# Inverse roots with fewer VectorE steps, row norms by halves on two engines, and two weight units of the odd layer split early into kept buffers

## The chip, the cores and the metric

The kernel runs on one core of one Trainium2 chip. The metric is the device time of an execution in microseconds (us), the median of three runs. The profile is of one further execution of the same kernel.

## The reference

The program is one inference step of a two-layer trunk, all in float32. It works on 128 context tokens (`x_prompt`) and 512 latent tokens (`x_sample`), each a row of 1024 values.

```
for l in 0, 1:
    six shift/scale/gate vectors from silu(c) for the latent rows, silu(c_ctx) for the context rows
    h = rms_norm(x, norm_mix_pre) * (1 + scale1) + shift1
    l = 0:  y = even_mixer(h)      # gated linear attention beside retention, one output projection
    l = 1:  y = mla_mixer(h)       # latent attention, 8 heads
    x = x + gate1 * rms_norm(y, norm_mix_post)
    h = rms_norm(x, norm_mlp_pre) * (1 + scale2) + shift2
    y = square(relu(h @ w_mlp1)) @ w_mlp2        # 1024 -> 4096 -> 1024
    x = x + gate2 * rms_norm(y, norm_mlp_post)

def rms_norm(x, g):
    return x * rsqrt(mean(x ** 2) + 1e-6) * g

def mla_mixer(h, ...):
    q_lat, ckv, kpe = split(h @ w_in_odd, (256, 256, 64))
    q   = rms_norm(q_lat, q_a_norm) @ w_q_b      # 8 heads of 128 + 64 (64 turned by position)
    ckv = rms_norm(ckv, kv_a_norm)               # keys and values: ckv @ w_kv_b, kpe
    ...                                          # cached keys joined, softmax, @ w_out_odd
```

It returns both sets of rows, the context's `ckv` and `kpe`, and the scan states.

## The kernel before

**Tiles.** The 640 token rows are five row tiles of 128; tile 0 is the context, tiles 1 to 4 are the latent rows. Activations `x`, `y` are 128x1024. The normed and modulated rows are turned on TensorE (`ps<-ident,y` in the trace) and kept as `hT`, 128 columns of tokens by eight blocks of 128 features (k-blocks).

**Products.** A float32 product is made of three: each operand is split into a high part (rounded to the type fp32r) and a low part (the rest), and `mm3` issues high by high, high by low, low by high. In the trace `hT_91` and `hT_92` are the two parts of the turned rows.

**Weights.** `plan` writes one list of all weight units, `wlist`, in the order in which they are wanted. `weights` walks it: for each unit it takes one of three load buffers (pool `raw`) and issues the load on SP's DMA queue. `weight_rooms` walks it behind, and takes a destination (usually from the pool `w` of ten buffers, otherwise what a `room` of the unit returns). `weight_split` then casts on ScalarE (high part), subtracts on VectorE (low part), and gives the load buffer back. A unit's `prio` goes to the thread that splits it.

**Order.** The `Weave` planner keeps many threads (Python generators), each recording operations through `Engine` at line 269, which is why every instruction of the trace has the line L269. While the program is written, the planner simulates the engines with its own costs per operation and picks for each engine the ready operation of the lowest `prio`; on VectorE the older thread goes first among equals, on the other engines the one that was ready first. The result is a fixed order per engine. A thread waits for an `Event`, or for a buffer of a `Slots` pool.

**PSUM.** Eight banks are lent between the slots `psg` (products) and `psum` (transposes) with `w.give`.

**Roots.** An inverse root is made of a logarithm and an exponential on ScalarE, and one Newton step of three VectorE operations (`rsqrt`). Ahead of it one VectorE operation adds the epsilon to the sum of squares.

**Norms.** `pre_norm` takes the squares of a tile (ScalarE), the root, writes the normed rows `xn` (VectorE; in the MLP's tail `xn` is the finished tile's `y` buffer), and starts two halves that each turn four blocks, modulate them into `h` (VectorE for half 0, ScalarE for half 1) and split `h` into `hT`. `residual` takes the root of the output's norm and adds into `x`. `out_proj` ends the mixer with the residual and the norm of each tile, and `mlp` ends with a `tail` per tile: two halves of the output added to `y`, squared, gated, then `residual`; after the first MLP `pre_norm` follows for the odd layer, after the second the result is stored.

**Odd layer.** `odd` has two groups of products with `w_in_odd`: 256 columns (query latents, `q_tile`) and 320 columns (keys, values and rotary key, `kv_tile`). Each group has four weight units of two k-blocks, `u_in_odd`, so that a tile takes 24 products per group. The second group's units go to buffers that `odd` opens (`room1`, `room2`); the first group's go to `w`. `norm256` norms a 256-column row of either group, and its result is turned. `park_x` stores each `x` tile when its `hT` is ready, and `cache` loads and turns the cached keys. Then `w_q_b`'s rotary part follows (`pqp` in the trace, `qpe_tile`), three banks go from `psg` to `psum`, and the heads begin: `projections` runs `proj(h)` for eight heads beside `all_values`, `scores`, `turns`, `outputs` and `finish`.

Of the kernel before, what the change touches and what calls it, by code (L numbers as in the profile page):

```python
# [19 lines left out]
P = 128  # L20
# [311 lines left out]
class Trunk:  # L332
# [68 lines left out]


# [75 lines left out]
    def weights(self):  # L478

        loads = [Event() for _ in self.wlist]  # L480
        self.w.spawn(self.weight_rooms(loads))
        for item, load in zip(self.wlist, loads):
            if isinstance(item, Event):
                continue
            if len(item) == 3:
                yield from self.pair_load(item[0], item[1], load)
                continue
            src, shape = item[:2]
            raw, hr = yield from self.take(self.raw, [P] + shape, F32, "raw")
            parts = list(src(raw) if callable(src) else [(raw, src)])  # L490
            self.w.aside(lambda: [self.nc.sync.dma_start(a, b) for a, b in parts],
                         then=lambda at: self.w.set(load, (raw, hr, at)))
            yield

    def weight_rooms(self, loads):
        for item, load in zip(self.wlist, loads):
            if isinstance(item, Event):
                yield item
                continue
# [21 lines left out]
    def wp_room(self):  # L521
        h = yield from self.take2(self.wp, [P, 2, 512], F32R, "wh")
        return h[0][0], h[1][0], [x[1] for x in h]

# [281 lines left out]
    def pre_norm(self, t, x, xn, sm, mods, ready, halves=None):  # L806
# [4 lines left out]
        nc.scalar.activation(self.junk, x, AF.Square, accum_out=sm[:, 0:1])  # L811
        yield
        nc.vector.tensor_scalar(sm[:, 1:2], sm[:, 0:1], D * EPS, None, op0=ALU.add)
        yield
        yield from self.rsqrt(sm[:, 1:2], sm[:, 2:3], sm[:, 3:4], 1.0 / D)
        nc.vector.tensor_scalar(xn, x, sm[:, 2:3], None, op0=ALU.mult)
# [40 lines left out]
    def residual(self, x, yg, sm, dst=None):  # L857

        nc = self.nc
        nc.vector.tensor_scalar(sm[:, 6:7], sm[:, 4:5], sm[:, 5:6], D * EPS, op0=ALU.add, op1=ALU.add)  # L860
        yield
        yield from self.rsqrt(sm[:, 6:7], sm[:, 7:8], sm[:, 3:4], 1.0 / D)
# [19 lines left out]
    def run(self):  # L882
# [17 lines left out]
        self.ident = const("ident", [P, P])  # L900
        self.fold, self.wide = const("fold", [P, P]), const("wide", [P, KC, 34])
# [8 lines left out]
    def plan(self):  # L910
# [11 lines left out]
        self.u_in_odd = (self.nat_units(io["w_in_odd"][0], ODD_GROUPS[:1], pair=True)  # L922
                         + self.nat_units(io["w_in_odd"][0], ODD_GROUPS[1:], rooms=self.odd_rooms))
# [36 lines left out]
    def main(self):  # L960
# [9 lines left out]
        halves = [[Event(), Event()] for _ in range(2)]  # L970

# [72 lines left out]
    def out_proj(self, units, oready, gate, mods, parked, gfree):  # L1044
# [6 lines left out]
        def tail(t):  # L1051
# [4 lines left out]
            for half in range(2):  # L1056
                ps, hp = yield out[half][t]
                s = slice(half * 512, half * 512 + 512)
                nc.scalar.activation(self.junk[:, 0:512], ps, AF.Square, accum_out=sm[:, 4 + half:5 + half])
                nc.vector.tensor_mul(y[:, s], ps, gr[c][:, s])  # L1060
                self.drop(hp)
# [32 lines left out]
    def mlp(self, ph, l, ready, xs, gate, mods, gfree):  # L1094
# [36 lines left out]
        def tail(t, ev):  # L1131
# [4 lines left out]
            for half in range(2):  # L1136
# [5 lines left out]
                nc.scalar.activation(self.junk[:, 0:512], y[:, s], AF.Square, accum_out=sm[:, 4 + half:5 + half])  # L1142
                yield
                nc.vector.tensor_mul(y[:, s], y[:, s], gr[c][:, s])
# [9 lines left out]
            else:  # L1154
                yield from self.residual(x, y, sm)
                yield from self.pre_norm(t, x, y, sm, mods, out_ready)
# [728 lines left out]
    def odd(self, ph, ready, xs):  # L1885
# [68 lines left out]
        def norm256(v, sm, gain, y):  # L1954
            nc.scalar.activation(self.junk[:, 0:256], v, AF.Square, accum_out=sm[:, 0:1])
            yield
            nc.vector.tensor_scalar(sm[:, 1:2], sm[:, 0:1], 256 * EPS, None, op0=ALU.add)
            yield
            yield from self.rsqrt(sm[:, 1:2], sm[:, 2:3], sm[:, 3:4], 1.0 / 256)
# [82 lines left out]
        for _ in range(3):  # L2042
            w.give(self.psum, (yield self.psg))
# [108 lines left out]
        def projections():  # L2152
            for h in range(HC):
                yield from proj(h)

# [150 lines left out]
        for g in (projections, all_values, scores, turns, outputs, finish, out_rooms):  # L2306
# [56 lines left out]
```

## Time and profile before

| what | value |
|---|---|
| median of three runs | 1523.9 us (1523.51 to 1525.08) |
| profiled execution, its own time | 1522.98 us |
| its span, first to last instruction | 1521.2 us |
| TensorE matmuls (PE) busy | 1473.8 us, 97% of the span, 8587 instructions |
| TensorE weight loads (PEld) busy | 1308.4 us, beside PE |
| VectorE (DVE) busy | 1092.6 us, 72% |
| ScalarE (ACT) busy | 651.7 us, 43% |
| GpSimd (POOL) busy | 113.0 us, 7% |
| mean granted TensorE clock | 0.987 |
| HBM traffic over the span | 112 GB/s |

Busy time counts instructions that run, not those that wait. In a row of the trace the first number is the start in us from the span's start, the second the time that the row's instructions took or covered; then come engine, line, operation, output and inputs with their shapes, and how often. A bracket at the end gives the idle time of that engine just before, and the operation whose end released it. SPq is the DMA queue of SyncE. "Granted clock" is the share of full clock that TensorE got.

### The profile page before, as it was taken

What the parts mean: (1) busy time and instruction counts of PE and PEld (TensorE: products, weight loads), DVE (VectorE), ACT (ScalarE), POOL (GpSimd) and SP (SyncE); (2) the same over time, 40 slices, a digit from 0 to 9 for tenths busy, and PEclk for the clock granted to TensorE, in tenths of its full rate; (3) what the DMA queues carried; (4) which work ended last, traced back from release to release, by engine and by line L of the source; (5) the groups of instructions that cost most, each with busy time, mean ns of one, the idle gap of its engine ahead of it and who ended that gap; (6) DMA issues with size and microseconds to landing.
All of it is one profiled execution on the core that took longest, in us unless ns stands there. A gap on an engine that the chain in (4) does not pass through costs nothing.

```text
span 1521.2 us, 22996 instructions
## 1 busy us (share of the span) xinstructions
PE 1473.8 (97%) x8587; PEld 1308.4 (86%) x8587; DVE 1092.6 (72%) x2247; ACT 651.7 (43%) x1526; POOL 113.0 (7%) x133
## 2 busy tenths in 40 slices
PE   5999999999999999999997999999999999999997
PEld 2688888889899899899896989997889989988996
DVE  4464674757767877777868788885765869996776
ACT  3583533646433232233246366673654323332332
POOL 0000200101021021021010100000002000000000
PEclk8999999999999999999998999999999999999999
DMA  9546222133555444445414110104422223432332
GB/s 331 166 156 209 87 69 80 44 110 112 163 163 152 143 128 146 144 129 152 123 42 140 48 29 22 43 29 139 167 83 70 63 77 112 130 120 84 98 103 105
DMA packets 148176, 171.44 MB, mean 113 GB/s; under 512 B 12144, under 2 KB 92640, under 8 KB 148064
## 3 DMA queue, kind: packets, MB, share of 16 engines
q1 hardware_dynamic: 148064, 169.97, 36.4%
q8 instruction: 67, 1.10, 0.3%
q14 instruction: 45, 0.37, 0.1%
HBM read 161.36 MB, written 8.59 MB: 112 GB/s over the span
## 4 chain that ended last, share of the span: by engine, by line
PE 89%; DVE 4%; ACT 3%; DMA 2%; issue 1%; SPq 0%; DVEq 0%; ACTq 0%
PE p L269 55%; PE pg L269 19%; PE ps L269 13%; PE pqk L269 2%; DVE y L269 1%; PE pv L269 1%; ACT junk L269 1%; DVE sm L269 1%; DMA raw<-in_w_in_even 1%; DVE x L269 1%; DMA x<-in_x_sample 1%; DMA raw<-in_w_out_odd 1%; ACT h L269 0%; SPq L269 0%; DVE rope L269 0%
## 5 line engine op out<-in xcount | busy, mean ns | idle before, releaser
L269 PE MATMUL p<-wh,hid 128*128 128x512 f32 x1280 | 399.6, 391 | 0.0
L269 PEld LDWEIGHTS p<-wh,hid 128*128 128x128 f32 x1280 | 240.3, 188 | 49.3
L269 PE MATMUL p<-hT,wh 128*128 128x256 f32 (+1 forms) x1280 | 280.1, 310 | 0.0
L269 PE MATMUL pg<-wh,hT 128*128 128x512 f32 (+3 forms) x840 | 264.8, 389 | 0.0
L269 PE MATMUL p<-wl,hid 128*128 128x512 f32 x640 | 249.7, 390 | 0.0
L269 DVE TENSOR_TENSOR wl<-raw,wh 128x1024 fp32r<-128x1024 f32 (+3 forms) x141 | 167.9, 1195 | 73.8 <-ACT wh L269 73.4
L269 PEld LDWEIGHTS p<-hT,wh 128*128 128x128 f32 x1280 | 216.1, 190 | 0.8
L269 ACT CAST wh<-raw 128x1024 fp32r<-128x1024 f32 (+3 forms) x145 | 147.6, 1022 | 137.9 <-PE p L269 98.6
L269 PE MATMUL p<-hT,wl 128*128 128x256 f32 (+1 forms) x640 | 198.7, 310 | 0.0
L269 PEld LDWEIGHTS pg<-wh,hT 128*128 128x128 f32 x840 | 155.2, 190 | 32.3 <-issue 9.2
L269 DVE SCALAR_TENSOR_TENSOR ada<-rada,cT,ada 128x512 f32<-128x512 f32 x196 | 146.7, 778 | 0.0
L269 PE MATMUL pg<-wl,hT 128*128 128x512 f32 (+3 forms) x360 | 141.9, 394 | 0.0
L269 PEld LDWEIGHTS p<-wl,hid 128*128 128x128 f32 x640 | 120.3, 188 | 24.1
L269 DVE TENSOR_TENSOR y<-y,p 128x512 f32<-128x512 f32 x140 | 96.0, 686 | 58.1 <-PE p L269 57.3
L269 POOL TENSOR_TENSOR r<-r 128x384 f32<-128x384 f32 (+1 forms) x80 | 80.6, 1007 | 729.1 <-ACT hid L269 392.8
L269 PEld LDWEIGHTS p<-hT,wl 128*128 128x128 f32 x640 | 121.3, 190 | 0.0
L269 ACT ACTIVATE r<-p 128x384 f32<-128x384 f32 (+1 forms) x80 | 35.0, 438 | 157.1 <-PE p L269 157.1
L269 PE MATMUL p<-hT,wq 128*128 128x320 f32 x576 | 88.1, 310 | 0.0
L269 PEld LDWEIGHTS p<-hT,wq 128*128 128x128 f32 x576 | 85.5, 188 | 0.5
L269 PEld LDWEIGHTS pg<-wl,hT 128*128 128x128 f32 x360 | 68.7, 191 | 11.9 <-issue 2.5
L269 DVE TENSOR_TENSOR hid<-r,hid 128x384 fp32r<-128x384 f32 (+1 forms) x80 | 38.9, 487 | 46.4 <-POOL r L269 46.3
L269 ACT CAST wq<-tw 128x512 fp32r<-128x512 f32 x48 | 27.6, 618 | 71.0 <-DVE tw L269 61.7
(282 smaller groups left out, 2325.0 us busy)
## 6 DMA issues: line engine op xcount, KB each, us to landing
raw<-in_w_mlp SPq DMA_DIRECT2D x128, 512.0 KB, 4.1
rada<-in_w_ada SPq DMA_DIRECT2D x160, 256.0 KB, 3.2
rada<-in_w_ada SPq DMA_DIRECT2D x16, 512.0 KB, 8.7
raw<-in_w_in_even SPq DMA_DIRECT2D x16, 512.0 KB, 4.9
x<-in_x_sample SPq DMA_DIRECT2D x8, 512.0 KB, 7.0
gate<-gate SPq DMA_DIRECT2D x8, 512.0 KB, 4.5
raw<-in_w_out_even SPq DMA_DIRECT2D x8, 512.0 KB, 5.2
raw<-in_w_out_odd SPq DMA_DIRECT2D x8, 512.0 KB, 3.7
```

Source lines behind the costliest of these rows:

```text
L269: emit = lambda: real(*a, **k)
```

## The change

**Roots.** A new `root(v, add, r, t)` takes the mean of squares and adds the epsilon as the bias of the logarithm. The two ScalarE operations follow the squares without a VectorE operation between them. The Newton step is three VectorE operations as before, each with two operators, and reads mean plus epsilon in its first one. `squares` scales the squares so that their sum is the mean. `pre_norm`, `residual` and `norm256` use it; other users of `rsqrt` stay. Where a row's squares come in two halves, the epsilon is added to the first half's sum as soon as that is there, and the sum serves as the second half's `add`.

**Halves.** In the first MLP's tail `pre_norm` runs with `shared=True`: VectorE writes columns 0 to 511 of the normed rows, ScalarE columns 512 to 1023.

**Kept buffers.** A new item `(2, kept)` of `wlist` stands ahead of unit 2 of the first odd group: `weights` takes two of the three load buffers there as destinations (named `wr`) and hands them to units 2 and 3 of that group, which pass through the third. They are given back when their group's last tile has used them. All eight units of the odd input projection have `prio=-1`.

**Banks.** The three banks that go from `psg` to `psum` ahead of the heads are now given by a thread of its own, once head 0's projections are done.

```diff
+    def root(self, v, add, r, t):
+        nc = self.nc
+        nc.scalar.activation(t, v, AF.Ln, bias=add)
+        nc.scalar.activation(r, t, AF.Exp, scale=-0.5)
+        yield
+        nc.vector.scalar_tensor_tensor(t, v, add, r, op0=ALU.add, op1=ALU.mult)
+        nc.vector.scalar_tensor_tensor(t, t, -0.5, r, op0=ALU.mult, op1=ALU.mult)
+        nc.vector.scalar_tensor_tensor(r, t, 1.5, r, op0=ALU.add, op1=ALU.mult)
+
+    def squares(self, x, sm, n):
+        self.nc.scalar.activation(self.junk[:, 0:x.shape[-1]], x, AF.Square, scale=n ** -0.5, accum_out=sm)
...
 # weights
+            if len(item) == 2:
+                for _ in range(item[0]):
+                    item[1].append((yield from self.take(self.raw, [P, 2, 2, 256], F32R, "wr")))
+                continue
...
+    def kept_room(self, kept):
+        t, held = kept.pop(0)
+        return t[:, 0], t[:, 1], [held]
+        yield
...
-    def pre_norm(self, t, x, xn, sm, mods, ready, halves=None):
+    def pre_norm(self, t, x, xn, sm, mods, ready, halves=None, shared=False):
-        nc.scalar.activation(self.junk, x, AF.Square, accum_out=sm[:, 0:1])
-        yield
-        nc.vector.tensor_scalar(sm[:, 1:2], sm[:, 0:1], D * EPS, None, op0=ALU.add)
-        yield
-        yield from self.rsqrt(sm[:, 1:2], sm[:, 2:3], sm[:, 3:4], 1.0 / D)
-        nc.vector.tensor_scalar(xn, x, sm[:, 2:3], None, op0=ALU.mult)
+        self.squares(x, sm[:, 0:1], D)
+        yield from self.root(sm[:, 0:1], self.eps, sm[:, 2:3], sm[:, 3:4])
+        if shared:
+            nc.vector.tensor_scalar(xn[:, 0:512], x[:, 0:512], sm[:, 2:3], None, op0=ALU.mult)
+            yield
+            nc.scalar.activation(xn[:, 512:D], x[:, 512:D], AF.Identity, scale=sm[:, 2:3])
+        else:
+            nc.vector.tensor_scalar(xn, x, sm[:, 2:3], None, op0=ALU.mult)
...
 # residual
-        nc.vector.tensor_scalar(sm[:, 6:7], sm[:, 4:5], sm[:, 5:6], D * EPS, op0=ALU.add, op1=ALU.add)
-        yield
-        yield from self.rsqrt(sm[:, 6:7], sm[:, 7:8], sm[:, 3:4], 1.0 / D)
+        yield from self.root(sm[:, 5:6], sm[:, 6:7], sm[:, 7:8], sm[:, 3:4])
...
 # plan
-        self.u_in_odd = (self.nat_units(io["w_in_odd"][0], ODD_GROUPS[:1], pair=True)
-                         + self.nat_units(io["w_in_odd"][0], ODD_GROUPS[1:], rooms=self.odd_rooms))
+        own = [Event() for _ in range(2)]
+        kept = []
+        for ev in own:
+            ev.at, ev.value = 0.0, lambda: self.kept_room(kept)
+        self.u_in_odd = (self.nat_units(io["w_in_odd"][0], ODD_GROUPS[:1], pair=True, rooms=[None, None] + own, prio=-1)
+                         + self.nat_units(io["w_in_odd"][0], ODD_GROUPS[1:], rooms=self.odd_rooms, prio=-1))
+        first = next(i for i, x in enumerate(self.wlist) if isinstance(x, tuple) and len(x) == 8 and x[6] is own[0])
+        self.wlist.insert(first, (2, kept))
...
 # tails of out_proj and mlp, for each half
+                if half == 0:
+                    nc.vector.tensor_scalar(sm[:, 6:7], sm[:, 4:5], EPS, None, op0=ALU.add)
...
 # mlp, tail of layer 0
-                yield from self.pre_norm(t, x, y, sm, mods, out_ready)
+                yield from self.pre_norm(t, x, y, sm, mods, out_ready, None, True)
...
 # odd, norm256
+            self.squares(v, sm[:, 0:1], 256)
+            yield from self.root(sm[:, 0:1], self.eps, sm[:, 2:3], sm[:, 3:4])
...
 # odd, ahead of the heads
-        for _ in range(3):
-            w.give(self.psum, (yield self.psg))
...
+        def banks():
+            yield proj_ev[0]
+            for _ in range(3):
+                w.give(self.psum, (yield self.psg))
...
-        for g in (projections, all_values, scores, turns, outputs, finish, out_rooms):
+        for g in (projections, all_values, banks, scores, turns, outputs, finish, out_rooms):
```

**What moves.** Names in the orders are the program's, with running numbers. The tiles' `y` buffers 0 to 4 are `y_3647`, `y_3651`, `y_3653`, `y_3655`, `y_3657` before, and `y_3639`, `y_3643`, `y_3645`, `y_3647`, `y_3649` after. `pg_7562` before and `pg_7560` after collect tile 0 of the first odd group; `pg_7622` is tile 1 of it, `pg_7561` after is tile 0 of the second group.

TensorE between the first MLP and the odd layer, before; `wp_7266`, `wp_7478`, `wp_7479` are units 1, 2 and 3 of the first group, `kdup` and `qpe` hold cached keys:

```order
L269 MATMUL pg_7562<-wp_7266,hT_92 128x256
L269 MATMUL ps_7590<-ident,y_3653 128x128
...
L269 MATMUL ps_7617<-ident,qpe_7542 128x128 x2
L269 MATMUL ps_7631<-ident,kdup_7561 128x128
L269 MATMUL ps_7639<-ident,y_3655 128x128
...
L269 MATMUL pg_7562<-wp_7478,hT_91 128x256 x2
L269 MATMUL pg_7562<-wp_7478,hT_92 128x256
...
L269 MATMUL ps_7686<-ident,y_3657 128x128
...
L269 MATMUL pg_7562<-wp_7479,hT_91 128x256 x2
L269 MATMUL pg_7562<-wp_7479,hT_92 128x256
```

The same place after; `wr_7213` and `wr_7268` are units 2 and 3, `wp_7550` and `wp_7598` units 0 and 1 of the second group:

```order
L269 MATMUL pg_7560<-wr_7213,hT_91 128x256
L269 MATMUL ps_7575<-ident,y_3645 128x128
...
L269 MATMUL pg_7561<-wp_7550,hT_91 128x320
...
L269 MATMUL pg_7560<-wr_7268,hT_92 128x256
L269 MATMUL pg_7622<-wp_7254,hT_91 128x256 x2
...
L269 MATMUL pg_7622<-wr_7268,hT_92 128x256
L269 MATMUL ps_7671<-ident,qpe_7543 128x128 x2
L269 MATMUL ps_7679<-ident,ql_7623 128x128 x2
L269 MATMUL pg_7561<-wp_7598,hT_91 128x320 x2
...
L269 MATMUL ps_7720<-ident,y_3647 128x128
```

Unit 2's products of tile 0 stood behind the transposes of tile 3 (`y_3655`) and unit 3's behind those of tile 4 (`y_3657`); now the 24 of tile 0, some of the second group and the 24 of tile 1 stand ahead of the transposes of tile 3 (`y_3647`).

VectorE before, around the low parts of units 2 and 3, where `x_3205` is tile 4's residual:

```order
L269 SCALAR_TENSOR_TENSOR x_3205<-y_3657,sm_3658,x_3205 128x1024
L269 TENSOR_TENSOR kpT_7548<-ps_7631,kpT_7547 128x128
L269 TENSOR_TENSOR hT_92<-h_7600,hT_91 128x512
L269 TENSOR_SCALAR h_7649<-ps_7639,mod_4782,mod_4206 128x128 x2
L269 TENSOR_SCALAR sm_3658<-sm_3658 128x1
L269 TENSOR_SCALAR h_7649<-ps_7639,mod_4782,mod_4206 128x128 x2
L269 TENSOR_TENSOR wp_7478<-raw_7221,wp_7478 128x512
L269 SCALAR_TENSOR_TENSOR sm_3658<-sm_3658 128x1
L269 TENSOR_TENSOR hT_92<-h_7651,hT_91 128x512
...
L269 TENSOR_SCALAR y_3657<-x_3205,sm_3658 128x1024
L269 TENSOR_TENSOR wp_7479<-raw_7283,wp_7479 128x512
```

VectorE after, around those two low parts; `p_` are banks of the first MLP's second product:

```order
L269 TENSOR_TENSOR y_3639<-y_3639,p_1124_7280 128x512
L269 TENSOR_TENSOR wr_7213<-raw_7274,wr_7213 128x512
L269 TENSOR_TENSOR y_3639<-y_3639,gate_93 128x512
L269 SCALAR_TENSOR_TENSOR sm_3642<-sm_3642 128x1
L269 TENSOR_TENSOR y_3643<-y_3643,p_1125_7299 128x512
L269 SCALAR_TENSOR_TENSOR sm_3642<-sm_3642 128x1 x2
L269 SCALAR_TENSOR_TENSOR x_2851<-y_3639,sm_3642,x_2851 128x1024
L269 TENSOR_SCALAR sm_3644<-sm_3644 128x1
L269 TENSOR_TENSOR y_3643<-y_3643,gate_94 128x512
L269 TENSOR_TENSOR wr_7268<-raw_7309,wr_7268 128x512
L269 TENSOR_TENSOR y_3643<-y_3643,p_1127_7320 128x512
```

The two subtractions moved from behind the residual of tile 4 to between the tail steps of tiles 0 and 1.

VectorE after, ahead of the residual of tile 4 (`x_3200`); `ql_7623` and `sm_7621` belong to the query norm of tile 0, `sm_3650` to tile 4's residual:

```order
L269 TENSOR_TENSOR y_3649<-y_3649,gate_94 128x512
L269 TENSOR_SCALAR h_7600<-ps_7575,mod_4774,mod_4198 128x128 x4
L269 SCALAR_TENSOR_TENSOR sm_7621<-sm_7621,eps 128x1
L269 SCALAR_TENSOR_TENSOR sm_3650<-sm_3650 128x1
...
L269 SCALAR_TENSOR_TENSOR ql_7623<-pg_7560,sm_7621,qpe_7543 128x256
L269 SCALAR_TENSOR_TENSOR x_3200<-y_3649,sm_3650,x_3200 128x1024
```

The query norm's root steps alternate with those of tile 4's residual, and its last operation stands ahead of it; in the order before, that norm stands behind the low part of unit 3.

VectorE at the end of the program, before; `y_11365` is the last tile, `sm_11366` its sums:

```order
L269 TENSOR_TENSOR y_11365<-y_11365,p_2311_15011 128x512
L269 SCALAR_TENSOR_TENSOR x_14873<-y_11363,sm_11364,x_14873 128x512
L269 TENSOR_TENSOR y_11365<-y_11365,gate_94 128x512
L269 TENSOR_SCALAR sm_11366<-sm_11366 128x1
L269 SCALAR_TENSOR_TENSOR sm_11366<-sm_11366 128x1
L269 TENSOR_SCALAR sm_11366<-sm_11366 128x1
L269 TENSOR_TENSOR sm_11366<-sm_11366 128x1
L269 SCALAR_TENSOR_TENSOR x_14883<-y_11365,sm_11366,x_14883 128x512 x2
```

And after:

```order
L269 SCALAR_TENSOR_TENSOR x_14850<-y_11341,sm_11342,x_14850 128x512
L269 TENSOR_TENSOR y_11343<-y_11343,gate_94 128x512
L269 TENSOR_TENSOR y_11343<-y_11343,p_2311_14989 128x512
L269 TENSOR_TENSOR y_11343<-y_11343,gate_94 128x512
L269 SCALAR_TENSOR_TENSOR sm_11344<-sm_11344 128x1 x3
L269 SCALAR_TENSOR_TENSOR x_14860<-y_11343,sm_11344,x_14860 128x512 x2
```

The last root's epsilon operation is gone from between the last gate product and the Newton step; the three steps of it are as many as before.

More of the change, by code (lines that the diff above doesn't have):

```diff
@@ L498, in weight_rooms @@
                 yield item
+                continue
+            if len(item) == 2:
                 continue
@@ L900, in run @@
         self.ident = const("ident", [P, P])
+        self.eps = const("eps", [P, 1])
         self.fold, self.wide = const("fold", [P, P]), const("wide", [P, KC, 34])
@@ L970, in main @@
         halves = [[Event(), Event()] for _ in range(2)]
+        nc.vector.memset(self.eps, EPS)
         for _ in range(2):
@@ L1058, in tail @@
                 s = slice(half * 512, half * 512 + 512)
-                nc.scalar.activation(self.junk[:, 0:512], ps, AF.Square, accum_out=sm[:, 4 + half:5 + half])
+                self.squares(ps, sm[:, 4 + half:5 + half], D)
                 nc.vector.tensor_mul(y[:, s], ps, gr[c][:, s])
+                if half == 0:
+                    nc.vector.tensor_scalar(sm[:, 6:7], sm[:, 4:5], EPS, None, op0=ALU.add)
                 self.drop(hp)
@@ L1141, in tail @@
                 yield
-                nc.scalar.activation(self.junk[:, 0:512], y[:, s], AF.Square, accum_out=sm[:, 4 + half:5 + half])
+                self.squares(y[:, s], sm[:, 4 + half:5 + half], D)
                 yield
+                if half == 0:
+                    nc.vector.tensor_scalar(sm[:, 6:7], sm[:, 4:5], EPS, None, op0=ALU.add)
                 nc.vector.tensor_mul(y[:, s], y[:, s], gr[c][:, s])
@@ L1954, in norm256 @@
         def norm256(v, sm, gain, y):
[L1955 to L1959, printed above, removed]
+            self.squares(v, sm[:, 0:1], 256)
+            yield from self.root(sm[:, 0:1], self.eps, sm[:, 2:3], sm[:, 3:4])
             nc.vector.scalar_tensor_tensor(y, v, sm[:, 2:3], gain, op0=ALU.mult, op1=ALU.mult)
```

## The prediction

> **What bounds the kernel now.** I read the page's first lines and its chain, then busy time by stage, then TensorE's rows wherever a stage showed it idle, and last VectorE, ScalarE and the DMA queue at those places.
>
> ```profile
> span 1521.2 us, 22996 instructions
> PE 1473.8 (97%) x8587; PEld 1308.4 (86%) x8587; DVE 1092.6 (72%) x2247; ACT 651.7 (43%) x1526; POOL 113.0 (7%) x133
> PE 89%; DVE 4%; ACT 3%; DMA 2%; issue 1%; SPq 0%; DVEq 0%; ACTq 0%
> ```
>
> TensorE is busy for all but 47.4 us, and 89% of the chain is its own. A change of norms and weight splits removes no matmul, so it can only pay where TensorE stands idle. By stage:
>
> ```profile
> 357.00:795.00 438.00, 437.78 (x2491) 400.28 (x2489) 324.29 (x499) 142.51 (x291) 66.47 (x64) 1.00 0.45 132
> 808.60:827.20 18.60, 8.47 (x48) 7.48 (x47) 15.73 (x44) 11.22 (x32) 0.00 (x0) 0.68 0.43 132
> 827.20:859.70 32.50, 32.50 (x241) 32.45 (x241) 23.07 (x81) 17.48 (x60) 0.76 (x3) 0.97 0.36 99
> 859.70:880.00 20.30, 18.18 (x111) 15.56 (x110) 16.20 (x51) 7.62 (x24) 4.25 (x9) 1.00 0.05 14
> 910.00:1010.00 100.00, 100.00 (x765) 99.47 (x765) 83.61 (x252) 67.75 (x214) 0.00 (x0) 1.00 0.09 26
> ```
>
> The columns are the stretch, its length, then busy time of PE, PEld, DVE, ACT, POOL, then the granted clock. The first MLP (357 to 795) and the attention heads (910 to 1010) are full: shorter roots there are worth nothing, TensorE covers them. The hole is 808.6 to 827.2, between the first MLP's last matmul and the odd layer: 10.1 us idle, at a clock of 0.68. TensorE there, row by row:
>
> ```profile
> 808.49 1.59 PE L269 MATMUL pg<-wp,hT 128*128 128x256 f32 x12
> 812.43 1.06 PE L269 MATMUL ps<-ident,y 128*128 128x128 f32 x8 [2.35 <-DVE y L269]
> 817.63 1.97 PE L269 MATMUL ps<-ident,y 128*128 128x128 f32 x8 [3.80 <-DVE y L269]
> 822.60 1.44 PE L269 MATMUL pg<-wp,hT 128*128 128x256 f32 x5 [2.79 <-DVE wp L269]
> 825.21 1.97 PE L269 MATMUL ps<-ident,y 128*128 128x128 f32 x8 [1.17 <-DVE y L269]
> 826.83 6.56 PE L269 MATMUL pg<-wp,hT 128*128 128x256 f32 x44
> 858.30 1.56 PE L269 MATMUL pg<-wh,hT 128*128 128x320 f32 x9
> ```
>
> TensorE does twelve products, half of row tile 0, and then has only transposes of tiles 2, 3 and 4 (`ps<-ident,y`) to wait for; the other half of tile 0 waits for weights (`DVE wp`). The reasons are on the other queues:
>
> ```profile
> 775.08 7.77 SPq L269 DMA_DIRECT2D raw<-in_w_in_odd  x3
> 803.89 0.62 ACT L269 CAST wp<-raw 128x512 fp32r<-128x512 f32 x1 [1.81 <-PE p L269]
> 811.53 0.75 DVE L269 TENSOR_SCALAR y<-x,sm 128x1024 f32<-128x1024 f32 x1
> 817.48 1.28 DVE L269 SCALAR_TENSOR_TENSOR x<-y,sm,x 128x1024 f32<-128x1024 f32 x1
> 819.99 1.05 ACT L269 ACTIVATE junk<-x 128x1024 bf16<-128x1024 f32 x1
> 821.87 0.68 DVE L269 TENSOR_TENSOR wp<-raw,wp 128x512 fp32r<-128x512 f32 x1
> 824.40 0.75 DVE L269 TENSOR_SCALAR y<-x,sm 128x1024 f32<-128x1024 f32 x1
> ```
>
> The third weight unit was asked for by 783, but its high part waits for a `w` buffer that the MLP's matmuls still read (803.89), and its low part is subtracted at 821.87, behind the norms of all five tiles.
>
> **The change, part by part.**
>
> *Weights split ahead.* The two late units now go to two of the three load buffers. Those come free when units 0 and 1 are split, about 782; the load (2.7 us, below) and the split put them at about 786 and 791, between steps of tile 0's tail. So from 808.6 TensorE can run all 24 products of tile 0 and of tile 1.
>
> ```profile
> raw<-in_w_in_odd SPq DMA_DIRECT2D x4, 320.0 KB, 3.2
> raw<-in_w_in_odd SPq DMA_DIRECT2D x4, 256.0 KB, 2.7
> 830.78 0.73 ACT L269 CAST wp<-raw 128x640 fp32r<-128x640 f32 x1
> 829.07 0.82 DVE L269 TENSOR_TENSOR wp<-raw,wp 128x640 fp32r<-128x640 f32 x1
> ```
>
> I follow the new order from 808.6 with the durations above: 0.133 us a 128x256 product (12 in 1.59), 0.156 a 128x320 product (9 in 1.40, up to the next row at 859.7), 0.9 to 1.1 for eight transposes. Tile 0: nine products to 809.8; then transposes of tile 2, whose ScalarE half comes at 810.6 (wait 0.7); fifteen more products, eight transposes and six products of the second group (0.9) to 814.4. Tile 1: 24 products to 817.6. Now VectorE holds it up: the root of the first query norm stands ahead of tile 4's residual in its order, and that norm's squares can't start before tile 0's products end at 814.4. ScalarE, in order, squares them (0.6), makes one h piece (0.35), squares tile 3's rows (1.05 and reading the sum), and only then gives the exponentials of the query norm and of tile 4's residual, 817.2. Six scalar steps of 0.13 and the query product (0.4) later, tile 4's residual starts at 818.4 (817.48 before). It takes 1.2, unit 1's split 0.7, smaller steps 1.9: tile 3's rows come out at 822.3, and tile 4's, after 1.8 of the same, at 824.1 (824.40 plus 0.75 before). TensorE waits 1.0 for the query rows, 1.4 for a low part of the second group, 1.0 for tile 3. Idle in all: 0.7 + 1.0 + 1.4 + 1.0 = 4.1 instead of 10.1.
>
> From 822.35 I take it as solid. The old solid stretch from 827.2 is 32.5 us. Less 28 first-group products (3.7), 12 of the second (1.9) and two transposes (0.3) that are already done, plus sixteen transposes (2.0) that are not, it is 28.6: the projections end at 850.9 instead of 859.7, 8.8 us earlier. That counts TensorE at full rate in the gaps. The trace says otherwise after long waits: eight transposes took 1.06 after 2.35 us of idleness, but 1.97 after 3.80 and again at 825.21; five products took 1.44 instead of 0.67, and the 44 that follow lost 0.5. Together 0.9 + 0.9 + 0.8 + 0.5 = 3.1 us of slow clock. The new waits are shorter but lie close together (3.4 idle within 4.8), so I charge 1.2 of it. [...]
>
> *The price of the kept buffers.* With two of three held until tile 4's products are done (about 833), the second group's units pass through one buffer: 3.2 for the load, 0.73 and 0.82 for the split, 4.8 each. Unit 1 is split at 820.3, so unit 2 at about 825 and unit 3 at 830. TensorE wants them at about 826.5 and 831.6. Slack 1.5, with other loads in the same queue: between nothing and 5, I charge 1.0. Queued behind unit 1's load, which waits for unit 0's split (810.8), are the cached key rows (needed 818.9), the gate rows (needed 200 us later) and the stores of x; `w_q_b` lands about 838 and is needed at 851.
>
> *Rows normed by halves.* No row shows 128x512 for this step. The 1024 form takes 0.75, and
>
> ```profile
> 886.49 0.54 DVE L269 TENSOR_SCALAR prob<-prob,sm 128x640 f32<-128x640 f32 x1
> 1513.59 0.63 ACT L269 ACTIVATE junk<-y 128x512 bf16<-128x512 f32 x1 [2.32 <-DVE y L269]
> ```
>
> a 640 form 0.54, so I take 0.48 by those two; ScalarE's half goes by its 512 form, 0.63. VectorE saves 0.27 five times, ScalarE pays 3.2 in all while it is busy 11.2 of 18.6. The order puts ScalarE's half of tile 2 behind two casts; that wait is the 0.7 above. Nothing further.
>
> *Shorter roots.* The epsilon step on VectorE goes, and the two exponentials follow the squares on ScalarE directly. Visible where nothing covers it, at the end:
>
> ```profile
> 1511.58 0.39 PE L269 MATMUL p<-wh,hid 128*128 128x512 f32 x1
> 1512.87 0.68 DVE L269 TENSOR_TENSOR y<-y,p 128x512 f32<-128x512 f32 x1
> 1514.12 0.19 ACT L269 ACTIVATION_READ_ACCUMULATOR junk<-y 128x1 f32 x1
> 1514.34 0.69 DVE L269 TENSOR_TENSOR y<-y,gate 128x512 f32<-128x512 f32 x1
> 1514.95 0.21 DVE L269 TENSOR_SCALAR sm<-sm 128x1 f32<-128x1 f32 x1
> 1515.19 0.44 ACT L269 ACTIVATE sm<-sm 128x1 f32<-128x1 f32 x2 [0.88 <-DVE sm L269]
> 1515.66 0.22 DVE L269 SCALAR_TENSOR_TENSOR sm<-sm 128x1 f32<-128x1 f32 x1 [0.51 <-ACT sm L269]
> 1515.92 0.15 DVE L269 TENSOR_SCALAR sm<-sm 128x1 f32<-128x1 f32 x1
> 1516.30 1.41 DVE L269 SCALAR_TENSOR_TENSOR x<-y,sm,x 128x512 f32<-128x512 f32 x2
> ```
>
> Now ScalarE has the exponentials at 1514.33 + 0.44 = 1514.77, under the gate product, which frees VectorE at 1514.95. Three scalar steps follow: 0.26 each by the step at 1515.66, 0.18 by the one behind it; I take 0.70. The residual starts at 1515.65, 0.65 earlier, and the tail ahead of it gains 0.1 by its earlier exponentials: 0.75, between 0.3 and 1.0.
>
> At the start:
>
> ```profile
> 30.75 1.11 PE L269 MATMUL ps<-ident,xn 128*128 128x128 f32 x4 [2.70 <-DVE xn L269]
> 58.95 1.97 PE L269 MATMUL ps<-ident,xn 128*128 128x128 f32 x8 [3.77 <-ACT h L269]
> ```
>
> the first wait loses one 0.3 us step that now stands behind the norm in VectorE's order; the second hangs on weights from memory. I take 0.3, between nothing and 0.7.
>
> *Banks given back later.* The three PSUM banks return after head 0's projections. TensorE idles 2.1 us in 859.7 to 880, where transposes (three banks now instead of six) and projections (five instead of two) share them: from 2.1 better to 2.1 worse, 0 taken.
>
> **Sum.** 8.8 - 1.2 - 1.0 + 0.75 + 0.3 = 7.65 us. The profiled execution took 1522.98 (span plus 1.8), 0.9 below the median of 1523.9; so 1515.3 for it, 1516.2 for the median. A difference under 0.2% (3 us) is about what a measurement of this kernel can't tell from none.
>
> **Rivals.**
> - *Given back at the heads.* TensorE comes 6.6 us earlier, but the rotation of the queries is VectorE's, busy 16.2 of 20.3 us there. If it can't come earlier, up to 6 us return: 1520 to 1522. For it: VectorE is busy 15.7 of 18.6 in the hole. Against: it idles 9.4 of 32.5 in the stretch between and needs some 6 of these back.
> - *More than forecast.* No slow clock (1.2), units in time (1.0), and 1.5 of the idle time at the heads gone through the banks: 3.7 more, 1512.5. [...]
> - *Slower: the single load buffer starves the second group.* Place: the DMA queue, where unit 2 stands behind the gate rows and unit 3 behind a store. A held queue is on record:
>
> ```profile
> 800.51 12.72 SPq L269 DMA_DIRECT2D gate<-gate  x2
> ```
>
> If unit 3 comes 12.7 late, at 843, TensorE stands still 11.4 us: 1527.6. It decides against the change from about 839 on. Against it: the gate rows wait for VectorE's last gate product, 814, well ahead of unit 2's turn at 820.
> - *It does nothing.* The kept units are split as late as before, since their casts wait for something else: only the ends gain, 1522.9. The freed buffers at 782 speak against it.
>
> **Chances.** Forecast, 1514 to 1519: 0.55. More: 0.20. Given back: 0.15. Slower: 0.06. Nothing: 0.04. The range leaves out the last two, the upper half of the giving back and the far end of the gain: 1511.5 to 1521. Faster by over 0.2% is 0.55 + 0.20 + two thirds of 0.15, 0.85; the same is the last third and the 0.04, 0.09; slower 0.06.
>
> **What would show it.** Right: 48 products of the first group before tile 3's transposes, two `wr` splits near 790, waits of about 4 us in the hole, the solid stretch ending near 851 to 853, the last residual 3.6 us behind the end of the last matmul instead of 4.3. Wrong: a wait for `raw` loads in the second group, VectorE rows of the query norms holding tile 4 longer than 824, or TensorE idle over 5 us between the projections and head 1.

## The result and the profile after

| | before | changed |
|---|---|---|
| median, us | 1523.7 (1522.59 to 1525.08, 4 runs) | 1513.55 (1513.27 to 1514.53, 4 runs) |
| ratio, 95% interval | 1 | 0.9935 (0.9923 to 0.9948) |
| profiled execution | 1522.98, span 1521.2 | 1513.64, span 1511.9 |

In a later group on one chip (label e9) the changed kernel had 1515.86 against 1523.84, ratio 0.9942 (0.9930 to 0.9955). So its medians lie 8 to 10 us below those of the kernel before (7 to 12 by the intervals); 7.7 was forecast, at 1516.2. Both medians lie in the forecast's range of 1511.5 to 1521. But 1513.55 lies just below the 1514 to 1519 that had the chance of 0.55, in the part called "more"; 1515.86 lies inside it. One execution of e1 (below), at 1900.56 us, was slow and is left out of its median.

The page after, first lines and chain:

```profile
span 1511.9 us, 22935 instructions
PE 1472.6 (97%) x8587; PEld 1304.5 (86%) x8587; DVE 1083.3 (72%) x2218; ACT 658.2 (44%) x1531; POOL 114.4 (8%) x133
PE 92%; DVE 3%; DMA 2%; ACT 1%; SPq 1%; issue 1%; DVEq 0%; ACTq 0%
```

TensorE does the same 8587 matmuls in 1.2 us less busy time. Most of the 9.3 us between the two spans is idle time: 47.4 us of the span before, 39.3 now. Busy time by stage, in the columns of the prediction's windows. The first row is the hole's stretch after, the next two run from the odd layer's first product to the first product of the queries' rotary part, before and after, and the last two from there to head 4's first product:

```profile
808.60:827.20 18.60, 15.24 (x105) 14.15 (x104) 16.66 (x49) 15.05 (x44) 0.00 (x0) 0.91 0.50 153
808.49:859.70 51.21, 41.09 (x287) 40.04 (x286) 38.91 (x125) 28.81 (x92) 0.76 (x3) 0.87 0.39 111
809.31:853.22 43.91, 39.98 (x288) 38.34 (x286) 34.06 (x108) 29.55 (x91) 0.76 (x3) 0.96 0.48 142
859.70:929.98 70.28, 66.87 (x465) 63.40 (x463) 58.62 (x179) 41.33 (x131) 4.25 (x9) 1.00 0.07 20
853.22:920.90 67.68, 66.08 (x464) 63.25 (x463) 57.65 (x178) 41.78 (x132) 4.06 (x9) 1.00 0.08 21
```

I call the first of these stretches P (projections, 51.21 to 43.91) and the second H (heads 0 to 3, 70.28 to 67.68). These two carry 9.9 us. TensorE's rows in P that waited, with two rows of products to compare (809.31 and 823.89):

```profile
809.31 1.56 PE L269 MATMUL pg<-wp,hT 128*128 128x256 f32 x12
818.49 0.41 PE L269 MATMUL ps<-ident,ql 128*128 128x128 f32 x2 [1.26 <-ACT wp L269]
820.32 0.56 PE L269 MATMUL pg<-wp,hT 128*128 128x320 f32 x2 [1.28 <-DVE wp L269]
822.25 1.56 PE L269 MATMUL ps<-ident,y 128*128 128x128 f32 x7 [0.81 <-DVE y L269]
823.89 2.05 PE L269 MATMUL pg<-wp,hT 128*128 128x256 f32 x8
833.09 0.41 PE L269 MATMUL pg<-wh,hT 128*128 128x320 f32 x1 [0.26 <-DVE wh L269]
844.79 0.30 PE L269 MATMUL ps<-ident,ql 128*128 128x128 f32 x1 [0.31 <-DVE ql L269]
```

Eight products take 2.05 us where twelve took 1.56 at 809.31: the granted clock was 0.50 there (822.72 to 826.13, last section). VectorE's rows on which the hand-made chain rested, the two split units first, then tile 4's residual and the rows of tiles 3 and 4:

```profile
786.47 0.69 DVE L269 TENSOR_TENSOR wr<-raw,wr 128x512 fp32r<-128x512 f32 x1
791.44 0.69 DVE L269 TENSOR_TENSOR wr<-raw,wr 128x512 fp32r<-128x512 f32 x1
818.26 1.27 DVE L269 SCALAR_TENSOR_TENSOR x<-y,sm,x 128x1024 f32<-128x1024 f32 x1
821.72 0.48 DVE L269 TENSOR_SCALAR y<-x,sm 128x512 f32<-128x512 f32 x1
823.43 0.49 DVE L269 TENSOR_SCALAR y<-x,sm 128x512 f32<-128x512 f32 x1
```

The first three were forecast to start at 786, 791 and 818.4, the last two to be done at 822.3 and 824.1; these two were done at 822.20 and 823.92. The end of the program after, TensorE's last row first:

```profile
1503.28 0.39 PE L269 MATMUL p<-wh,hid 128*128 128x512 f32 x1
1505.75 0.69 DVE L269 TENSOR_TENSOR y<-y,gate 128x512 f32<-128x512 f32 x1 [0.85 <-ACT junk L269]
1506.36 0.60 DVE L269 SCALAR_TENSOR_TENSOR sm<-sm 128x1 f32<-128x1 f32 x3
1506.99 1.41 DVE L269 SCALAR_TENSOR_TENSOR x<-y,sm,x 128x512 f32<-128x512 f32 x2
```

The last residual starts 3.71 us behind the last matmul's start; before it was 4.72 (1511.58 to 1516.30). And the start, the first rows of tile 0 and the first product of the first mixer:

```profile
19.48 0.69 PE L269 MATMUL ps<-ident,xn 128*128 128x128 f32 x2 [5.31 <-DVE xn L269]
35.03 0.77 PE L269 MATMUL pg<-wh,hT 128*128 128x480 f32 x1
```

Before, three batches of modulation products ran at 12.84, 14.98 and 19.02 and that transpose at 20.07; the mixer's first product stood at 33.66. So the mixer starts 1.4 us later.

### The profile page after: what moved, and what is told of

Its sections match the earlier page's. It is cut to its first block, busy times and chain, and to the rows that moved or that the text cites. A ratio compares the mean times of both kernels' runs of the same rounds, so it can differ in the third digit from the quotient of the medians.

```text
span 1511.9 us, 22935 instructions
## 1 busy us (share of the span) xinstructions
PE 1472.6 (97%) x8587; PEld 1304.5 (86%) x8587; DVE 1083.3 (72%) x2218; ACT 658.2 (44%) x1531; POOL 114.4 (8%) x133
## 4 chain that ended last, share of the span: by engine, by line
PE 92%; DVE 3%; DMA 2%; ACT 1%; SPq 1%; issue 1%; DVEq 0%; ACTq 0%
PE p L269 57%; PE pg L269 19%; PE ps L269 13%; PE pqk L269 2%; SPq L269 1%; PE pv L269 1%; DMA rada<-in_w_ada 1%; DVE sm L269 1%; DMA raw<-in_w_out_odd 1%; DMA x<-in_x_prompt 1%; DVE y L269 0%; DVE rope L269 0%; DMA kr<-in_state_ret 0%; DVE x L269 0%; ACT prob L269 0%
## 5 line engine op out<-in xcount | busy, mean ns | idle before, releaser
L269 DVE TENSOR_TENSOR wl<-raw,wh 128x1024 fp32r<-128x1024 f32 (+3 forms) x141 | 167.9, 1194 | 75.9 <-ACT wh L269 67.4
```

Of the source, the lines that this page charges most:

```text
L269: emit = lambda: real(*a, **k)
```

## The experiments

Each kernel's profile is cut at the same five instructions. "Start" is the time of the first mixer's first product, "odd" of the odd layer's first; P and H are as above, "end" runs from the last matmul's end to the span's end. Times in us, medians with the number of runs, ratio to the kernel before with its interval. A profile is of one execution, up to 2.3 us from its kernel's median (e1's took 1513.88, e2's 1519.11, e6's 1517.66, e9's 1513.99), so the stretches show where time goes and not by how much two medians differ. Kernels e1 to e4, e5 to e8 and e9 to e12 shared a chip, on which the kernel before had 1523.56, 1523.19 and 1523.84.

| kernel | start | odd | P | H | end | median | ratio |
|---|---|---|---|---|---|---|---|
| before | 33.66 | 808.49 | 51.21 | 70.28 | 9.23 | 1523.7 (4) | 1 |
| changed | 35.03 | 809.31 | 43.91 | 67.68 | 8.23 | 1513.55 (4) | 0.9935 (0.9923 to 0.9948) |
| e1 kept buffers alone | 34.01 | 807.38 | 43.40 | 69.87 | 9.55 | 1516.18 (5) | 0.9950 (0.9937 to 0.9964) |
| e2 all but kept buffers | 34.98 | 809.90 | 47.06 | 69.33 | 8.17 | 1520.83 (12) | 0.9986 (0.9977 to 0.9994) |
| e3 late banks alone | 34.33 | 808.75 | 51.99 | 69.35 | 9.17 | 1523.16 (12) | 0.9997 (0.9988 to 1.0007) |
| e4 first root old | 34.49 | 808.48 | 43.77 | 67.91 | 8.50 | 1513.55 (5) | 0.9933 (0.9922 to 0.9945) |
| e5 all but late banks | 35.58 | 811.19 | 43.62 | 70.45 | 8.23 | 1517.85 (5) | 0.9963 (0.9949 to 0.9977) |
| e6 all but halves | 35.30 | 812.50 | 43.99 | 68.25 | 8.24 | 1515.94 (5) | 0.9955 (0.9943 to 0.9968) |
| e7 all but roots | 35.02 | 808.99 | 45.60 | 69.34 | 9.23 | 1517.47 (6) | 0.9967 (0.9956 to 0.9979) |
| e8 all small norms late | 34.86 | 810.79 | 40.68 | 70.71 | 8.24 | 1514.77 (5) | 0.9946 (0.9933 to 0.9958) |
| e9 changed, again | 35.16 | 809.12 | 44.67 | 67.66 | 8.19 | 1515.86 (5) | 0.9942 (0.9930 to 0.9955) |
| e10 = e4, again | 34.22 | 807.31 | 43.39 | 67.93 | 8.44 | 1512.97 (5) | 0.9927 (0.9914 to 0.9941) |
| e11 e4, two norms late | 34.53 | 809.23 | 40.93 | 67.38 | 8.17 | 1509.27 (4) | 0.9902 (0.9889 to 0.9916) |
| e12 kept, banks, last root | 34.47 | 808.66 | 44.88 | 71.18 | 8.36 | 1517.35 (5) | 0.9952 (0.9939 to 0.9964) |

**e1, the kept buffers alone.** The kernel before with the `plan`, `weights` and `kept_room` hunks of the diff.

> The kernel before with one part of the change alone: units 2 and 3 split early into kept load buffers, all eight units at prio -1; old roots, whole rows on VectorE, banks given back as before. Theory (the early split is what closes the hole): the products of the odd layer's projections end about 7 us earlier against the end of the first MLP, as in the changed kernel (7.3), and nothing else moves: 1516 to 1517.5. Rival (the rows come early enough only with the shorter roots and the halves): TensorE waits for tiles 3 and 4 nearly as long as before, 7 us idle of the old 10.1, and the gain is under 4: 1520 or more.

P fell by 7.8 us, no less than in the changed kernel (7.3), and the median lies in the theory's range. Early splits by themselves do in the hole what the whole change does.

**e2, the changed kernel without them.**

```diff
-  ODD_GROUPS[:1], pair=True, rooms=[None, None] + own, prio=-1)
+  ODD_GROUPS[:1], pair=True)
-  self.wlist.insert(first, (2, kept))
```

> The changed kernel without the kept buffers (units 2 and 3 through the w pool, prio 1 as before); new roots, halves and later banks stay. Theory: the hole stays, 8 to 10 us idle between the first MLP and the odd layer; what is left is the end (1.0), the heads (2.5) and the start (0.8 worse): 1520.5 to 1521.5. Rival (roots and halves carry the hole): 1516 to 1518.

The time is the theory's, the place is not quite: P still fell by 4.15. TensorE's rows that waited in its hole:

```profile
817.03 1.97 PE L269 MATMUL ps<-ident,y 128*128 128x128 f32 x8 [5.15 <-DVE y L269]
821.55 0.48 PE L269 MATMUL ps<-ident,y 128*128 128x128 f32 x1 [1.08 <-DVE y L269]
822.73 1.76 PE L269 MATMUL ps<-ident,y 128*128 128x128 f32 x7 [0.70 <-ACT y L269]
```

6.9 us of waits instead of 10.1, and none for weights. Faster norms (roots and halves, which this run doesn't tell apart) fill part of the hole by themselves; beside the early splits (7.8 alone) that adds nothing (7.3 together). The parts compete for the same idle time and their gains don't add.

**e3, the late banks alone.**

```diff
-        for _ in range(3):
-            w.give(self.psum, (yield self.psg))
+        def banks():
+            yield proj_ev[0]
+            for _ in range(3):
+                w.give(self.psum, (yield self.psg))
```

> The kernel before with the three banks given back after head 0's projections and nothing else changed. Theory (the banks are the 2.5 us that TensorE gained between the projections and head 2, where I had put 0): 1521 to 1522, TensorE's waits between 865 and 895 fall from 3.3 us to about 1.5. Rival (the gain at the heads comes with the shorter query and key norms or with the earlier arrival): 1523.3 to 1524, waits there as before.

H fell by 0.9 of the 2.6. TensorE's waits in it stayed nearly as they were (3.06 us in all, 3.26 before), as the rival said, and the time can't be told from none. The longer P (51.99) goes with a lower granted clock, 0.84 against 0.87 before.

**e5, the changed kernel without them.** The diff of e3 turned round, on the changed kernel.

> The changed kernel with the three banks given back ahead of the heads, as before. Theory (late banks are the gain at the heads, but only beside the other parts, since alone they gave 0.9 us): from the first rotary product of the queries to head 3 TensorE needs 48 to 49 us again instead of 46.3, and the time is 1515 to 1516.2. Rival (earlier queries and shorter norms are the gain): 46.3 to 46.9 us there, time within 0.6 of the changed kernel's 1513.55.

H is 70.45, 2.8 us more, so without the late banks the other parts gain nothing at the heads. To head 3's first product it took 51.20 us, past the theory's 49. The median, 1517.85, is above the theory's range; in its profile the odd layer began 1.9 us later than in the changed kernel, which the banks don't touch. The first rows of TensorE that waited in H, in e5 and then in the changed kernel:

```profile
864.87 0.42 PE L269 MATMUL pqk<-qlT,wp 128*128 128x384 f32 x1 [0.37 <-DVE rope L269]
867.91 0.35 PE L269 MATMUL pv<-wp,ckT 128*128 128x256 f32 x1 [0.75 <-DVE rope L269]
872.50 0.44 PE L269 MATMUL ps<-ident,qs 128*128 128x128 f32 x2 [1.37 <-DVE qs L269]
```

```profile
869.02 0.44 PE L269 MATMUL ps<-ident,qs 128*128 128x128 f32 x2 [1.11 <-DVE qs L269]
870.64 0.30 PE L269 MATMUL ps<-ident,qs 128*128 128x128 f32 x1 [0.36 <-DVE qs L269]
```

With three banks given away early, head 0's products (`pqk`, `pv`) wait for VectorE's rotation of the queries (`rope`), which reads the banks of the products before. With the banks kept they don't. These rows make 1.0 us of the 2.8 (waits of 2.49 against 1.47). The rest is later idle time, 0.6, and busy time for the same products, 67.19 against 66.08; its cause is not shown.

**e6, the changed kernel without halves.** `pre_norm(..., out_ready)` instead of `(..., out_ready, None, True)`.

> The changed kernel with whole rows normed on VectorE in the first MLP's tail. Theory (halves only shift work to ScalarE, which is as full there, so they bring nothing): from the first odd product to the first rotary product 43.5 to 44.3 us, as with them (43.9), and 1513.2 to 1514.1. Rival (each of the five rows is 0.27 us later, and tiles 3 and 4 carry it to TensorE): 44.5 to 45.3 us, 1514.4 or more.

P is 43.99, as with halves (43.91 and 44.67) and as the theory said, and H 0.6 more. The median has the rival's time, but not for the rival's reason: in its profile, of the slowest of its five executions, the excess lies ahead of P (odd at 812.50), where halves do nothing. They bring nothing that these runs can tell.

**e7, the changed kernel with the old roots.** The `root` and `squares` hunks undone, `rsqrt` and its epsilon steps back.

> The changed kernel with the old inverse roots everywhere; kept buffers, halves and late banks stay. Theory (the roots pay at the end alone and cost a little elsewhere): the stretch between first MLP and heads as in the changed kernel within 0.5 us, the end 1.0 us longer (9.2 from the last matmul to the span's end instead of 8.2), the first even projection near 34.1 instead of 35.0, the stretch from output projection to second MLP 0.75 shorter; in sum the same time, 1513 to 1514.5. Rival (the roots carry part of the hole): first odd product to first rotary product 46 us or more, 1516 or more.

My theory fell. The end is 1.0 longer as expected, but P is 0.9 to 1.7 longer (0.9 against e9, whose granted clock in P was 0.92; over the whole execution e7 had 0.988 and e9 0.990; just below the rival's 46), H 1.7, and the median is past the rival's bound. Its longest wait in P is for the first query rows:

```profile
829.70 0.44 PE L269 MATMUL ps<-ident,ql 128*128 128x128 f32 x2 [2.18 <-DVE ql L269]
```

In this order the query rows are what is late next. That the longer root alone makes them late in P is not shown: e1 and e12 have early weights and the old root there too, their first query rows come without a wait, and their P is 43.40 and 44.88.

**e9, the changed kernel again.**

> The changed kernel once more, so that the three others of this group stand beside it on the same chip. Where the earlier groups' chips differ little, 1513.5 to 1514.5; if the chips set the stretch ahead of the first MLP's end, up to 1516.

Its 1515.86 is 2.3 above the first group's median. Its profile is of its fastest execution, 1513.99, and shows little of that: the odd layer begins no later (809.12), and P is 0.76 longer by its clock (0.92 in P, against 0.96; last section). What the other executions lost stays open.

**e4 and e10, the old root in the very first norm.**

```diff
+        if halves:   # the first mixer's norm
+            ...      # old squares, epsilon step, rsqrt
+        else:
             self.squares(x, sm[:, 0:1], D)
```

> The changed kernel with the old root in the very first norm alone (the rows that the first mixer reads). Theory (the shorter root made the planner put two transposes of the first tile ahead of modulation products, and TensorE stands 5.3 us at them for rows that come late from memory): the order at the start is the old one again, the first even projection starts near 33.7 instead of 35.0, and the time falls by 0.7 to 1.4: 1512.2 to 1512.9. Rival (the 0.8 us at the start is only when the loads happened to land): the first projection again anywhere between 33.5 and 35.5, time 1513.6 within 0.4.

> The changed kernel with the old root in the very first norm, beside the changed kernel on one chip. Theory (the shorter root there moves two transposes ahead of modulation products and costs): first even projection 0.6 to 1.2 us earlier, first odd product 0.8 to 2 us earlier, time 0.7 to 2 us below the changed kernel. Rival (the loads' landing alone): equal within 0.5.

Beside the changed kernel on one chip (e10 and e9) the mixer starts 0.9 us earlier and the odd layer 1.8; the medians differ by 2.9, but the intervals of the ratios overlap. e4's median, 1513.55, is just the changed kernel's first one, as the rival said, though from another group. The rows of e10 at the start:

```profile
13.64 3.90 PE L269 MATMUL ps<-rada,wide 128*32 128x512 f32 x8 [1.01 <-DMA rada<-in_w_ada]
19.71 1.05 PE L269 MATMUL ps<-rada,wide 128*32 128x512 f32 x4 [2.17 <-DMA rada<-in_w_ada]
20.69 0.82 PE L269 MATMUL ps<-ident,xn 128*128 128x128 f32 x3
34.22 0.59 PE L269 MATMUL pg<-wh,hT 128*128 128x480 f32 x1
```

The old order is back, and with it the start. The start differs between kernels with the same first norm too, and in these rows TensorE waits 1.01 and 2.17 us for loads: the eight kernels with the old first norm have it at 33.66 to 35.02, the six with the new one at 34.86 to 35.58. So the shift of the order is shown, its 0.9 us likely, and the time not settled.

**e8, all small norms late.** `w.spawn(q_tile(t), None, 1)` and the same for `kv_tile(t)`.

> The changed kernel with the threads of the query and key norms at prio 1, so that VectorE's order has tile 3's normed rows and tile 4's residual ahead of the first query norm. Theory (the 3.4 us of waits that are left in the hole, and the half clock behind them, come from VectorE's order, where the query root and tile 4's residual stand ahead of tile 3's rows): waits fall to 1 to 2 us, the clock stays full, the projections end 1.5 to 3 us earlier, 1510.5 to 1512. Rival (ScalarE, in order, holds the same steps, or the queries now come late for their product): the waits move and add up to 3 us or more, time within 0.7 of 1513.55 or above it.

P fell to 40.68, with waits of 2.2 us. That leaves 38.5 us of work, about what e11 (below) has at a granted clock of 1.00, 38.78. So the place of the small norms in the orders was the cause of what was left. The edit moves them on ScalarE as well as on VectorE; which of the two counts is not told apart. H rose by 3.0 (its first wait is 0.94 for `ckT`, the keys), and the time is no better, as the rival said.

**e11, two query norms late.** e4 with one line more:

```diff
-            w.spawn(q_tile(t))
+            w.spawn(q_tile(t), None, 1 if t < 2 else None)
```

> The kernel of the line above, with the query norms of tiles 0 and 1 alone at prio 1 (key norms and the later queries as in the changed kernel). Theory (the waits left in the hole are VectorE's order; all norms late lost 3 us at the heads because the keys of head 0 came late, which is not touched here): first odd product to first rotary product 40.7 to 41.5 us instead of 43.9, from there to head 4 67.7 to 69, in sum 1 to 3 us below the line above. Rival (the gain in the hole is given back at the heads, where the rotation of the queries on VectorE sets the time): both stretches together 111 to 112 as with all norms late, time as the line above.

P is in the theory's range, H just below its own, and the median 3.7 us below e10's instead of 1 to 3. Its P and H, and the waits at the place where the changed kernel lost 3.35 us and had a clock of 0.50 (two more, of 0.18 and 0.36, follow by 828):

```profile
809.23:850.16 40.93, 38.78 (x288) 37.04 (x286) 34.11 (x108) 29.56 (x92) 1.09 (x3) 1.00 0.53 153
850.16:917.54 67.38, 65.98 (x465) 63.19 (x464) 57.65 (x179) 41.46 (x131) 4.06 (x9) 1.00 0.08 21
```

```profile
817.55 0.41 PE L269 MATMUL pg<-wp,hT 128*128 128x320 f32 x1 [0.36 <-ACT wp L269]
818.46 0.71 PE L269 MATMUL pg<-wp,hT 128*128 128x320 f32 x3 [0.50 <-DVE wp L269]
823.79 0.44 PE L269 MATMUL ps<-ident,ql 128*128 128x128 f32 x2 [0.37 <-DVE ql L269]
824.81 1.00 PE L269 MATMUL pg<-wh,hT 128*128 128x320 f32 x5 [0.38 <-DVE wh L269]
```

The clock is 1.00 over the whole of P. At 1509.27 this is the fastest kernel of all, 0.9902 of the time before; its interval lies below that of the changed kernel beside it (e9). Against e10, from which it differs by the one line, the intervals overlap slightly, but its slowest execution (1510.95) is below e10's fastest (1511.66).

**e12, the kept buffers, the late banks and the last root alone.**

> The kernel before with the kept buffers and prio -1, the late banks, and the new root in the last residual alone (no other new roots, no halves). Theory (roots and halves elsewhere bring nothing that counts): as the kept buffers alone, 1.0 us less at the end and 0.5 to 1 less at the heads: 1513 to 1514.5 by this chip's changed kernel, level with it. Rival (the shorter roots of the query and key norms carry 2 to 3 us at the heads, as taking all roots out of the changed kernel showed): 1.5 to 3 us above it.

The median is 1.5 us above e9's, at the near end of the rival's range, but the intervals overlap, so the time doesn't decide. P is 44.88, though up to the hole it is e1 with the same waits; the last section tells why. H lost part of its time in one more slow stretch, behind waits of 0.90 and 1.09:

```profile
871.00:874.00 3.00, 2.69 (x13) 2.72 (x14) 0.30 (x2) 0.77 (x2) 0.00 (x0) 0.51 0.27 76
```

About 1.5 us of its 71.18 are this clock, an estimate from the 3.00 us at 0.51; without them H would still be 2 us above the changed kernel's. That agrees with e7: the roots of the small norms count at the heads.

Taken over all kernels, H is 67.4 to 68.3 in the six profiles where kept buffers, late banks and short small roots are together without e8's edit (the changed kernel, e4, e6, e9, e10, e11), and 69.3 or more in e8 and in the seven that lack at least one of them. So the gain at the heads belongs to the three together, and no share of it can be put on one.

## Why the prediction was right, point by point

- *Place and mechanism.* Right. The hole was where the time was, and the chain of the new order came out within half a microsecond at each point shown above. The rows by halves took 0.48 on VectorE, as estimated, and 0.71 on ScalarE instead of 0.63.
- *Projections, 8.8 less 1.2 and 1.0, so 6.6.* Measured 7.3 here and 6.5 in e9. Inside it, the waits were 3.35 instead of 4.1 (none for tile 2). The slow clock cost up to 1.7 and not 1.2, an estimate from the 3.41 us at a granted clock of 0.50 in the last section. The single load buffer cost 0.26 and not 1.0; its rival of 1527.6 never came near, and nothing was given back at the heads.
- *The clock.* That short waits lying close together would slow it was right: behind 1.26, 1.28 and 0.81, none near 3.80, it was 0.50 from 822.72 to 826.13. The 1.2 charged for it was my estimate, and too small. Slow products "after long waits" was an incomplete reading of the kernel before: its wait of 3.80 ran from 813.83 to 817.63, and the clock fell at 815.18, when that wait was 1.35 us old (last section).
- *Banks, 0 taken, 2.1 either way.* Mis-sized. H gained 2.6. Taking out the late banks costs 2.8 (e5), but taking out the roots costs 1.7 (e7) and the kept buffers 1.65 (e2), so the banks are needed for it and don't carry it alone. Of the three parts of the rival "more than forecast", two came true, the units in time and the heads; the third didn't, since the clock did slow.
- *The end, 0.75.* Measured 1.0, its upper end: 9.23 to 8.23.
- *The start, a gain of 0.3.* Wrong in sign: the odd layer began 0.82 later. I costed the removed step and not the order. With a shorter root the planner puts two transposes ahead of modulation products that would have been ready; the rows come no earlier from memory (their squares, which wait for them, start at 16.28 before and 16.29 after), and TensorE stands 5.31 us behind them.
- *Roots elsewhere.* "Worth nothing" was said of the first MLP and the heads from 910 on, and no run shows a gain there. But the sum had no term for the roots of the query and key norms, and without them the first heads lose 1.7 (e7). In P, e7's 0.9 to 1.7 can't be put on them (e1).
- *Left out.* From head 4 to the last matmul the changed kernel takes 0.78 longer (581.99 to 582.77). No run ties it to one part: it is absent in e1 and e3 and there in the others, 0.45 or more. It stays open.

The profile's sum is 0.82 - 7.30 - 2.60 + 0.78 - 1.00 = -9.30, the difference of the spans. The forecast 7.65 had three terms too small (banks 2.6, projections 0.7, end 0.25) and two missing losses (1.1 at the start against the forecast, 0.78 later). The errors, 3.55 and 1.9, partly cancel, so that the sum came within 1.7 is in part luck; that the projections came within 0.7 is not.

## What to carry to other kernels

When several edits aim at one stretch of idle time, price them together: early weights alone took 7.8 us from it, faster norms 4.15, both 7.3. When an order is planned from costs, a cheaper operation also moves others, and what counts is the queue it ends up ahead of; here one such move likely cost the start 0.9 us, and another (two norms behind the rows that TensorE waited for) was worth 2.5 in P. After an edit that fills a hole, look for what is late next, and check the clock row before blaming instructions.

## What the runs showed of the hardware

The slow stretches measured here were 3.41, 6.83 and 13.65 us long, at a granted clock of 0.50. e1 and e12 have one order on TensorE in the hole, with the same three waits (e1, then e12):

```profile
815.51 0.41 PE L269 MATMUL pg<-wp,hT 128*128 128x320 f32 x1 [0.53 <-ACT wp L269]
816.37 0.42 PE L269 MATMUL pg<-wp,hT 128*128 128x320 f32 x1 [0.33 <-DVE wp L269]
820.01 1.97 PE L269 MATMUL ps<-ident,y 128*128 128x128 f32 x8 [2.29 <-DVE sm L269]
```

```profile
816.80 0.42 PE L269 MATMUL pg<-wp,hT 128*128 128x320 f32 x1 [0.52 <-ACT wp L269]
817.66 0.41 PE L269 MATMUL pg<-wp,hT 128*128 128x320 f32 x1 [0.33 <-DVE wp L269]
821.30 1.97 PE L269 MATMUL ps<-ident,y 128*128 128x128 f32 x8 [2.29 <-DVE sm L269]
```

Their windows of 8 us around the slow stretch, where the granted clock is the third number from the end (e1, then e12):

```profile
818.72:826.72 8.00, 6.71 (x45) 6.71 (x46) 7.01 (x25) 5.27 (x14) 0.00 (x0) 0.79 0.59 200
```

```profile
820.00:828.00 8.00, 6.70 (x35) 6.70 (x36) 6.14 (x24) 5.17 (x14) 0.00 (x0) 0.58 0.56 195
```

The window from 820.00 to 828.00 has 0.79 in the changed kernel and 0.57 in e9, where the slow stretches below are 3.41 and 6.83 us long. By these two I estimate 3.4 us at half speed for e1 (8 x 0.21 x 2) and 6.7 for e12. Narrow windows find the edges. Below are the 3.41 us ahead of the fall and then the whole slow stretch, in the kernel before, the changed kernel and e9:

```profile
811.77:815.18 3.41, 1.39 (x11) 1.18 (x11) 3.04 (x10) 2.74 (x10) 0.00 (x0) 1.00 0.38 71
815.18:828.83 13.65, 7.24 (x31) 6.65 (x32) 10.69 (x30) 6.63 (x19) 0.00 (x0) 0.50 0.55 184
```

```profile
819.30:822.71 3.41, 1.57 (x9) 1.23 (x10) 3.41 (x14) 3.08 (x11) 0.00 (x0) 1.00 0.41 96
822.72:826.13 3.41, 3.41 (x18) 3.41 (x17) 3.41 (x12) 2.39 (x5) 0.00 (x0) 0.50 0.50 198
```

```profile
816.74:820.15 3.41, 0.87 (x7) 0.44 (x5) 3.16 (x11) 3.41 (x13) 0.00 (x0) 1.00 0.79 253
820.15:826.98 6.83, 6.71 (x28) 5.97 (x29) 6.22 (x22) 4.86 (x13) 0.00 (x0) 0.50 0.44 140
```

The slow stretches are 13.65, 3.41 and 6.83 us long, and the kernel before had one more of 6.83, from 57.42 to 64.25, also at 0.50. Within 0.01 us these are four, one, two and two times 3.41; why is not shown. In the 3.41 us ahead of these three falls TensorE was not idle throughout, but busy for 1.39, 1.57 and 0.87 us.

So one order with the same three waits (e1, e12), or one program in two executions (changed, e9), had a slow stretch of about 3.4 us or of about 6.8. At 0.50 that costs up to half its length, 1.7 or 3.4 us by estimate, and P differs with it: 43.40 and 44.88, 43.91 and 44.67. In e9 the slower products also filled the changed kernel's third wait, 0.81, so its P grew by 0.76 only. In e9 the stretch began 2.57 us earlier than in the changed kernel (820.15 and 822.72), while its odd layer began only 0.2 earlier. What ended e1's slow stretch after about 3.4 us and kept e9's for 6.83 is not shown. These pairs differ in P by 1.48 and 0.76 us with the same order on TensorE in the hole, so differences of that size between two profiles of this case can't be put on an edit without their clock rows.
